# A hybrid HGRN2, attention and mixture-of-experts layer: the scheduler orders each engine's instructions by its detailed time model

## The chip, the cores and the metric

The kernel runs on one core of one Trainium2 chip. The metric is the device time of one execution in microseconds (us), the median over the runs shown. Engines: PE is TensorE's matmuls and PEld its weight loads, DVE is VectorE, ACT is ScalarE, POOL is GpSimd, SP is SyncE, which here issues almost all DMAs.

## The reference, cut to what matters

One layer over 256 latent tokens, with 256 context tokens as a prefix, and a width of 1024, in float32:

```python
u_lat = modulate(rmsnorm(x, g[0]), m_lat[0], m_lat[1])      # m = silu(c) @ w_mod + b_mod
y_lat = token_mixer(u_lat, u_ctx, ...)                       # HGRN2 (8 heads, 2 directions) and attention
x = x + m_lat[2] * rmsnorm(y_lat, g[1])
t = modulate(rmsnorm(x, g[2]), m_lat[3], m_lat[4])
logits = t @ router_w + router_b                             # top 4 of 32 experts, softmax over the 4
for e in range(N_EXPERTS):
    h = t @ w_up[e] + b_up[e]                                # 1024 -> 2048
    a = glu * sigmoid(1.702 * glu) * (lin + 1.0)             # both clamped at 7
    out = out + combine[:, e:e + 1] * (a @ w_down[e] + b_down[e])
x = x + m_lat[5] * rmsnorm(out, g[3])
```

The token mixer projects latent and context tokens by `w_in` (1024 x 8704), runs the recurrence and the attention, gates the two results, and multiplies by `w_branch` and `w_out`. Each expert's weights are 8 MB up and 4 MB down; all 32 are read once.

## The kernel before

The program is written as straight Python code over tiles, and is traced in that order. Three stages follow one another.

**The mixer.** Weights come in slabs of 1 MB (`slab`, L224, its transfer at L227) into three buffers with the tag `raw`. ACT and DVE split each half of a slab into a high and a low float32r part (L239, L240; two buffers, tag `hl`), and PE multiplies high by high, high by low and low by high (`mm3`, L247, L250, L251). Small dependent chains run between these: the gates and the scan of a pair of HGRN heads (`hgrn_pair`, four times), and the heads of the attention (`attn_head`, eight times: scores, maximum on DVE, exponential on ACT at L675, a product on DVE at L677, transposes on PE at L680, a split again). Between the heads stand the gated branches (`branch`: a sigmoid on ACT at L699). ACT has one table of functions at a time; where the function's table is not the one it holds, an ACT_TABLE_LOAD stands ahead of the instruction.

**Routing.** The last product with `w_out` leads through the second norm, the logits, the top 4 and the position of each token in its expert's list (L804 to L832).

**The experts.** Four experts at a time, the chosen tokens (64 at most for each) are gathered by a one-hot product (`gather`, L918, L922). For expert e, `up` loads four pieces of 2 MB (`wu`, L887, seven buffers over three tags) and multiplies (L953 for the bias, L963: 64 matmuls), then the gate is computed on DVE and ACT (L939 to L943). `down` of the expert before loads four pieces of 1 MB (`wd`, L894, six buffers) and multiplies (L990: 32 matmuls), copies on ACT (L993) and adds into the accumulators on PE (L997). `transposed` turns the gate's result (L977 on PE, L979 on ACT), and `scatter_weights` makes the weights of the sum (L931, L933, L935). The loop in program order:

```python
for e in range(NE - 1):
    a = up(e, xe, part if e == 0 else None)
    ...
    if before is not None:
        down(e - 1, before)
    before = transposed(e, a)
    if e % 4 == 3: ...          # gather the next four
down(NE - 2, before)
with tc.If(state["most"] > CAP): ...      # L1020: experts with more than 64 tokens, not taken here
e = NE - 1
row_bcast(g3, misc, mod[:, 0, 40:48], gT[:, 24:32], "b")     # L206 on DVE, L208 on PE, L214 on ACT
aT = transposed(e, up(e, xe))
```

Behind the branch comes expert 31, ahead of it in program order a row broadcast of the last gain (`row_bcast`), and then the last norm and the output.

**What sets the order.** Leaving `with tile.TileContext(nc)` starts the scheduler. It simulates the traced program on a model of the machine; whenever an engine's queue can take another instruction, it gives it the ready one that stands earliest in the program, and a tile gets a buffer when one of its tag is free. The order that comes out of this simulation is fixed in the program; on the chip every queue runs in that order and waits on semaphores. What is inside `tc.If` is one unit, and nothing is moved across it. `tc.keep_in_program_order` pins a few instructions (some first matmuls of a group, and the preloads of ACT's tables at L125). So a model of time decides only which ready instruction goes first.

## Time and profile before

| | us |
|---|---|
| median of 3 runs | 1460.55 (1459.64 to 1463.08) |
| the profiled execution | 1461.97 |
| its span, first to last instruction | 1460.4 |
| PE busy in the span | 1361.9 (93%) |
| DVE, ACT busy | 506.3, 360.6 |
| read from HBM | 479.15 MB |

The span is what the profile shows; 1.57 us of the execution's own time lie around it. Start times in the rows are us from the start of the span, durations of single instructions in the groups are ns. A row's bracket tells how long the engine sat idle before it, and what ended that.

### The profile page before, as it was taken

How to read it: one execution, taken by the hardware profiler on the slowest of the kernel's cores; microseconds unless marked ns; L12 is line 12 of the kernel's file. 1: busy time of each engine (PE TensorE's matmuls, PEld its weight loads, DVE VectorE, ACT ScalarE, POOL GpSimd, SP SyncE). 2: the span in 40 equal slices, each digit the busy share in tenths (PEclk: the TensorE clock that was granted, in tenths of full speed). 3: DMA queues.
4: the chain of work that ended last, by engine and by line, in shares of the span. 5: the costliest groups of instructions: out<-in, count | busy, mean ns of one | idle time of the engine just before them, and what ended most of it. 6: DMA issues, size and time to landing. Idle time of an engine off the chain costs nothing. (4 is left out here: it accounts for less than half of the span.)

```text
span 1460.4 us, 18959 instructions
## 1 busy us (share of the span) xinstructions
PE 1361.9 (93%) x8151; PEld 762.6 (52%) x8151; DVE 506.3 (35%) x916; ACT 360.6 (25%) x648; POOL 4.2 (0%) x16
## 2 busy tenths in 40 slices
PE   6999999999999999999999999999999999999976
PEld 3789788898899844553333333333333333333322
DVE  4688877778865521111111110111011111101012
ACT  5445444456554410100010010011010110101001
POOL 0000000000000000000000000000000000000000
PEclk9999999999999999999999999999999999999998
DMA  9544343246659599999999999999999999999992
GB/s 343 169 140 150 118 145 110 70 145 231 221 203 343 220 341 391 427 426 425 423 426 426 426 423 424 426 426 425 423 427 424 426 424 425 427 424 425 424 407 88
DMA packets 97553, 481.53 MB, mean 330 GB/s; under 512 B 6692, under 2 KB 57352, under 8 KB 63160
## 3 DMA queue, kind: packets, MB, share of 16 engines
q1 hardware_dynamic: 96560, 479.25, 81.8%
q8 instruction: 66, 1.08, 0.3%
q10 hardware_dynamic: 776, 0.84, 0.2%
q14 instruction: 23, 0.19, 0.0%
q0 software_dynamic: 128, 0.16, 0.0%
HBM read 479.15 MB, written 1.08 MB: 329 GB/s over the span
## 5 line engine op out<-in xcount | busy, mean ns | idle before, releaser
L963 PE MATMUL pu<-wu,xe 128*64 128x512 f32 x2048 | 450.5, 595 | 0.0
L963 PEld LDWEIGHTS pu<-wu,xe 128*64 128x64 f32 x2048 | 162.9, 137 | 270.0 <-issue 246.3
L990 PE MATMUL py<-wd,aT 128*64 128x512 f32 x992 | 231.2, 599 | 0.0
L939 DVE TENSOR_SCALAR gl<-pu 128x512 f32<-128x512 f32 (+1 forms) x33 | 22.2, 675 | 485.7 <-PE pu L963 485.7
L990 PEld LDWEIGHTS py<-wd,aT 128*64 128x64 f32 x992 | 65.7, 136 | 117.5 <-issue 108.9
L940 ACT ACTIVATE sg<-gl 128x512 f32<-128x512 f32 (+1 forms) x33 | 20.2, 616 | 416.9 <-DVE gl L939 416.9
L997 PE MATMUL acc<-ysb,cw 64*128 64x512 f32 x248 | 61.6, 615 | 16.1 <-ACT ysb L993 15.4
L918 PE MATMUL pgx<-oh,xt 128*128 128x256 f32 x256 | 66.7, 400 | 9.1 <-ACT aT L979 4.4
L918 PEld LDWEIGHTS pgx<-oh,xt 128*128 128x128 f32 x256 | 44.9, 195 | 39.2 <-issue 19.3
L931 DVE TENSOR_SCALAR ow<-iota,posb,comb 128x128 f32<-128x128 f32 x64 | 19.5, 344 | 132.1 <-PE pcw L933 132.1
L922 DVE TENSOR_SCALAR xe<-pgx,aff,mod 128x256 f32<-128x256 f32 x32 | 17.4, 544 | 127.2 <-PE pgx L918 127.2
L247 PE MATMUL pf<-uh,hlf 128*128 128x512 f32 x128 | 51.8, 410 | 3.1 <-ACT hlf L239 3.1
L979 ACT COPY aT<-pat 128x512 f32<-128x512 f32 x32 | 18.8, 586 | 143.6 <-PE pat L977 143.2
L251 PE MATMUL pf<-uh,hlf 128*128 128x512 f32 x128 | 52.8, 414 | 0.1
L250 PE MATMUL pf<-ul,hlf 128*128 128x512 f32 x128 | 51.9, 406 | 0.0
L997 PEld LDWEIGHTS acc<-ysb,cw 64*128 64x128 f32 x248 | 21.3, 186 | 52.4 <-ACT ysb L993 37.4
L993 ACT COPY ysb<-py 128x512 f32<-128x512 f32 x31 | 18.2, 586 | 117.6 <-PE py L990 117.6
L977 PEld LDWEIGHTS pat<-ident,gl 128*128 128x128 f32 x128 | 19.8, 205 | 46.0 <-issue 34.9
L977 PE MATMUL pat<-ident,gl 128*128 128x128 f32 x128 | 30.6, 327 | 12.0 <-DVE gl L943 12.0
L247 PE MATMUL pga<-uh,hlga 128*128 128x256 f32 x128 | 36.9, 288 | 1.7 <-ACT hlga L239 1.7
L251 PE MATMUL pga<-uh,hlga 128*128 128x256 f32 x128 | 36.3, 284 | 1.0 <-DVE hlga L240 1.0
L247 PE MATMUL pv<-hli,uh 128*128 128x256 f32 x128 | 36.5, 285 | 0.0
(387 smaller groups left out, 2142.7 us busy)
## 6 DMA issues: line engine op xcount, KB each, us to landing
wu<-in_w_up_dram SPq DMA_DIRECT2D x128, 2048.0 KB, 27.3
wd<-in_w_down_dram SPq DMA_DIRECT2D x124, 1024.0 KB, 18.4
wm<-in_w_mod_dram SPq DMA_DIRECT2D x16, 1024.0 KB, 4.9
wm<-in_w_mod_dram SPq DMA_DIRECT2D x16, 512.0 KB, 10.2
wf<-in_w_in_dram SPq DMA_DIRECT2D x8, 1024.0 KB, 5.2
wga<-in_w_in_dram SPq DMA_DIRECT2D x8, 1024.0 KB, 5.2
wwb<-in_w_branch_dram SPq DMA_DIRECT2D x8, 1024.0 KB, 6.4
wi<-in_w_in_dram SPq DMA_DIRECT2D x4, 1024.0 KB
```

The costliest lines, as they stand in the source:

```text
L247: i = pe.matmul(o, a[0], b[0], start=k == 0 and opens, stop=False)
L250: pe.matmul(o, a[0], b[1], start=False, stop=False)
L251: pe.matmul(o, a[1], b[0], start=False, stop=k == KT - 1 and closes)
L918: pe.matmul(pg, pairs(xt[:, tt], k), oh[:, tt].rearrange("p e s -> p (e s)"), start=tt == 0, stop=tt == 1)
L931: dve.tensor_scalar(ow[:, tt], view(iota, [[0, 2], [1, CAP]]), posb[:, tt, e:e + 1], comb[:, tt, e:e + 1], op0=ALU.is_equal, op1=ALU.mult)
L939: dve.tensor_scalar(gl, glu_ps, 7.0, None, op0=ALU.min)
L940: act.activation(sg, gl, AF.Sigmoid, scale=1.702)
L963: pe.matmul(pu[i][hf * CAP:(hf + 1) * CAP], lhs, wt[:, k % 2, i * 1024 + hf * 512:i * 1024 + (hf + 1) * 512], start=False, stop=k == KT - 1)
L977: pe.transpose(pt[:, b * P:(b + 1) * P], pairs(a[:], b), ident)
L979: act.copy(aT.rearrange("p a b -> p (a b)"), pt)
L990: pe.matmul(py[n * CAP:(n + 1) * CAP], aT[:, k % 4, (k // 4) * CAP:(k // 4 + 1) * CAP], wt[:, i, n * 512:(n + 1) * 512], start=k == 0, sto ...
L997: pe.matmul(acc[tt][n], cw[r, tt * P:(tt + 1) * P], ysb[r], start=False, stop=False)
```

## The change

One argument is given to the tile context. The simulation that orders the instructions then runs on the library's detailed model in place of its plain one. The detailed model lets transfers share the DMA engines, follows TensorE's clock, and treats the parts of an instruction (issue, read, write-back, the way of a semaphore) apart; it counts every table of ACT as loaded. No instruction, tile, buffer count or size in the kernel's text is changed; the order of every engine's queue, SP's and POOL's among them, may be.

```diff
-    with tile.TileContext(nc) as tc:
+    with tile.TileContext(nc, schedule_with_timeline_sim=True) as tc:
         hybrid_layer(tc, *args)
```

## Rows read from the trace of the kernel before

**Rows 1.** The page: busy time of each engine, then 40 slices of the span.

```profile
PE 1361.9 (93%) x8151; PEld 762.6 (52%) x8151; DVE 506.3 (35%) x916; ACT 360.6 (25%) x648; POOL 4.2 (0%) x16
...
GB/s 343 169 140 150 118 145 110 70 145 231 221 203 343 220 341 391 427 426 425 423 426 426 426 423 424 426 426 425 423 427 424 426 424 425 427 424 425 424 407 88
```

**Rows 2.** Windows: busy us (x instructions) of each engine, clock, DMA share, GB/s.

```profile
27.00:500.00 473.00, 462.84 (x4072) 412.81 (x4073) 348.28 (x558) 235.89 (x406) 2.21 (x5) 0.99 0.51 175
300.00:400.00 100.00, 93.94 (x728) 88.70 (x727) 82.69 (x140) 60.45 (x116) 0.00 (x0) 1.00 0.60 202
480.00:500.00 20.00, 20.00 (x164) 19.27 (x164) 9.83 (x15) 8.32 (x23) 0.00 (x0) 1.00 0.33 115
500.00:514.00 14.00, 10.63 (x53) 6.67 (x52) 11.01 (x51) 8.03 (x22) 0.49 (x1) 1.00 0.86 311
514.00:553.00 39.00, 38.83 (x168) 18.61 (x168) 5.74 (x12) 5.10 (x8) 0.50 (x1) 1.00 0.94 353
553.00:600.00 47.00, 47.00 (x220) 23.45 (x218) 6.54 (x12) 4.13 (x8) 0.00 (x0) 1.00 0.96 400
560.00:1410.00 850.00, 796.03 (x3590) 303.24 (x3586) 116.10 (x212) 86.10 (x160) 0.00 (x0) 1.00 1.01 425
```

**Rows 3.** Timeline of PE, second expert, then expert 30 and its neighbours.

```profile
539.69 14.11 PE L963 MATMUL pu<-wu,xe 128*64 128x512 f32 x64
...
1372.65 13.95 PE L963 MATMUL pu<-wu,xe 128*64 128x512 f32 x64
1386.44 1.89 PE L990 MATMUL py<-wd,aT 128*64 128x512 f32 x8
...
1393.06 0.44 PE L933 MATMUL pcw<-ident,ow 128*128 128x128 f32 x2 [0.73 <-ACT aT L979]
```

**Rows 4.** Groups of PE, 560 to 1410 us: busy, mean ns, idle before, releasers.

```profile
L977 PE MATMUL pat<-ident,gl 128*128 128x128 f32 x120 | 29.0, 329 | 9.9 <-DVE gl L943 9.9
...
L933 PE MATMUL pcw<-ident,ow 128*128 128x128 f32 x60 | 13.1, 300 | 14.6 <-ACT aT L979 14.6
```

**Rows 5.** DMA issues of the page, then waits of PE, 500 to 1410 us.

```profile
wu<-in_w_up_dram SPq DMA_DIRECT2D x128, 2048.0 KB, 27.3
wd<-in_w_down_dram SPq DMA_DIRECT2D x124, 1024.0 KB, 18.4
...
PE acc L997 <- ACT ysb L993: 15.4, 21, 0.7
```

**Rows 6.** Timeline of SP near the end, then the tile wu's landing, 1300 to 1410 us.

```profile
1347.38 5.29 SPq L887 DMA_DIRECT2D wu<-in_w_up_dram  x2
...
DMA to landing us min/median/max: 27.9/29.5/30.0
```

**Rows 7.** Timeline behind the branch: DVE, then PE.

```profile
1408.53 1.02 PE L997 MATMUL acc<-ysb,cw 64*128 64x512 f32 x4
...
1414.67 1.29 DVE L206 TENSOR_TENSOR rbdb<-ident,rbcb 128x512 f32<-128x512 f32 x2 [25.28 <-PEq L1020]
...
1415.42 3.78 PE L208 MATMUL rbpb<-rbdb,ones 128*128 128x512 f32 x4 [5.87 <-DVE rbdb L206]
...
1419.13 1.06 PE L953 MATMUL pu<-bu,sel 96*64 96x512 bf16 x4
```

**Rows 8.** Timeline of ACT at the start, then its groups, 330 to 430 us.

```profile
9.10 1.28 ACT L220 ACT_TABLE_LOAD   x1
...
10.39 0.48 ACT L220 ACTIVATE rs<-ssq,epsc 128x1 f32<-128x1 f32 x2
...
24.70 1.58 ACT L300 ACTIVATE xnT<-xnT,mod,aff 128x256 f32<-128x256 f32 x3 [0.99 <-DVE aff L295]
26.19 1.03 ACT L239 CAST hlf<-wf 128x1024 fp32r<-128x1024 f32 x1
...
L699 ACT ACT_TABLE_LOAD x4 | 5.1, 1283 | 0.1
L675 ACT ACT_TABLE_LOAD x3 | 3.8, 1283 | 0.1
```

## The prediction, made before the changed kernel was built

> **What bounds the kernel now.** I began with the page. PE is busy 93% of the span, and from slice 17 of 40 on the read rate stands at 423 to 427 GB/s [rows 1]. The first half is therefore PE's, and in the second two resources may run level, so stages are read next, by windows [rows 2]. From 27 to 500 us PE is busy 462.84 of 473 us. That leaves 10.16 us of gaps, and in the worst 100 us of it 6.06. DVE and ACT have 348.28 and 235.89 us of work there, so they have room to be served in another order. From 500 to 514 us PE is busy 10.63 of 14 us and DVE 11.01: a short dependent chain. From 560 to 1410 us the read rate is 425 GB/s at a DMA share of 1.01, with PE busy 796.03 of 850 us. The granted clock is 0.99 to 1.00 wherever it is listed, so I take the duration of a matmul as fixed.
>
> Which of the two bounds the experts is settled by the timeline of PE. The second expert's up-product begins at 539.69 us and expert 30's at 1372.65 [rows 3]; 832.96 / 29 = 28.72 us for each. The transfers of one expert, four of 2048 KB and four of 1024 KB [rows 5], are 12.58 million bytes, which at 425 GB/s take 29.6 us. PE thus runs a little faster than its weights come and eats up a lead of about 29 x 0.9 = 25 us. How much is left? The last two pieces of expert 30 are issued by 1347.38 + 5.29 = 1352.67 us, and such a piece lands 29.5 us later (median) [rows 6], at 1382.2. PE comes to the last of four pieces at about 1372.65 + 0.75 x 13.95 = 1383.1 [rows 3]. So **the lead is gone just when the loop ends**: 0.9 us are left. This is the reading on which the forecast turns. A wait taken out of PE's loop gains about 1 us in all, as the weights then come last; a wait put in costs its whole length, for every expert.
>
> **The change part by part.** It removes no instruction and adds none except, perhaps, table loads of ACT, which follow from the order. What it moves is the place of any instruction in its queue. Which ones move, the trace of before cannot show, so each stage is bounded from both sides. The sum stands against the profiled execution, 1461.97 us, which is 1.42 above the median of 1460.55. I call changes under 0.2%, 2.9 us, no difference, about what a measurement of this kernel can tell.
>
> *Start, ahead of 27 us.* ACT runs the last products of the normalization up to 26.19 us, then the cast that the first projection waits for, 1.03 us [rows 8]. If the cast goes ahead of them, PE can start up to 1 us earlier; if another such cast gets in front, 1 us later. I take 0 (-1.0 to +1.0).
>
> *The mixer, 27 to 500 us.* No reorder gains more than PE's 10.16 us of gaps [rows 2]. At worst I let all of it run at the rate of its worst stretch: 473 x 6.06 / 100 = 28.7 us of gaps, so 28.7 - 10.2 = +18.5. An order made with a finer model should see the short chains (score, exponential, product, transpose) with truer lengths and fill a quarter of the gaps: **-2.5**, near the gain's end since 98% of the stretch is full already and small errors of order are absorbed by DVE's 125 us and ACT's 237 us of idle time.
>
> *The transition, 500 to 514 us.* One chain; at most 14 - 10.63 = 3.4 us to gain or, taken the same, to lose [rows 2]. I take 0. A chain has one order.
>
> *SP's and POOL's queues.* Both may be reordered. SP's weights leave when a buffer comes free: the rate of 115 GB/s from 480 to 500 us, with 353 behind it [rows 2], I read as buffers still held by the mixer, which program order decides and time does not. POOL has 2.21 us of work in the mixer and small transfers. I take 0 for both. If the mixer gave its buffers up early enough to keep the stream at 425 GB/s from 514 on, 39 x (1 - 353/425) + 47 x (1 - 400/425) = 6.6 + 2.8 = 9.4 us more lead would be there.
>
> *The experts.* PE's largest waits are for the copy of the down-product (15.4 us, up to 0.7 each), for the copy of the transposed gate (14.6) and for the gate (9.9) [rows 4, 5]. Putting other matmuls in front of the waiting ones would hide them. The gain is the lead, 0.9, say **-1.1** with the earlier end of the copies (at best -1.1 - 9.4 = -10.5, with the stream kept full). A loss: one more wait per expert for an ACT copy, 0.73 us as in the timeline [rows 3], for 31 experts: +22.6. Queued behind such a wait is everything of PE, 64 up-matmuls first. I stay near the gain, as each wait of this kind is already in the order of before, so the model must find a second one.
>
> *Behind the branch.* PE ends its last sum at 1408.53 + 1.02 = 1409.55 us and stands for 5.87 us, as DVE comes to the row broadcast at 1414.67, released by the branch on PE's queue. Then PE runs the broadcast for 3.78 us ahead of expert 31's first matmul at 1419.13 [rows 7]. The up-product does not need the broadcast. With it behind, PE could start when DVE now does: 1419.13 - 1414.67 = up to 4.4 us gained. A model of time in which DVE's product and its semaphore take longer would let the bias matmuls, ready at once, go first. Half of it: **-2.2** (-4.4 to 0).
>
> *ACT's tables.* From 330 to 430 us ACT loads tables seven times, 1283 ns each, in front of sigmoids (L699) and exponentials (L675) in turn; at 9.10 us the next instruction starts 1.29 us behind such a load's start, at its end [rows 8]. The detailed model takes every table as held, so nothing in it keeps exponentials together. I take 0 for my forecast and price the rest as a rival. The Trainium skill, "ScalarE: Activation LUTs", section "What ACT_TABLE_LOAD costs", gives about 1.28 us for the load and a drain of about 1.38 us with it, 2.66 us for each switch; by it each added load would cost twice what I use. The trace shows the load and no gap behind it at 9.10 us [rows 8], so the trace decides here.
>
> The sum: 0 - 2.5 + 0 - 1.1 - 2.2 = -5.8; 1461.97 - 5.8 = 1456.2 for a profiled execution, and 1460.55 - 5.8 = **1454.8** for the median.
>
> **The rivals.**
>
> *One more wait for each expert* (0.22). Place: between PE and ACT in the loop, at the copies of L979 and L993. If the detailed model has the weights come later than they do, PE stands idle in the simulation, so it is given the transposes and sums the moment they are ready. On the chip, where the weights are there, PE then reaches them early and waits. For it: the lead falls to 0.9 us, so a model even slightly slower at transfers finds the loop bound by them throughout. Against it: such waits are in the order of before already, 0.7 us each [rows 5]. Price: 31 x 0.73 = 22.6, giving 1460.55 + 22.6 = 1483. It decides the sign from 5.8 + 2.9 = 8.7 us on, 0.28 us for each expert, since it first has to undo my other gains.
>
> *Exponentials and sigmoids in turn* (0.16). Place: ACT's queue in the eight heads and branches. If each head's exponential ends up between sigmoids of the branches, there are up to 16 loads in place of 7: 9 x 1.283 = 11.6 us of ACT. ACT is busy 60.45 of 100 us there, so half of it may be hidden from PE: about +6, giving 1466. For it: the loads already alternate, 4 and 3. Against it: PE's order there is mostly filled by slab products, which need no table. The rule of the Trainium skill, "ScalarE: Activation LUTs", section "Table sets: the hidden batching unit", that work is to be grouped by table set speaks for this rival; no run here shows yet what an order blind to them does.
>
> *No change that counts* (0.22). The two models may give nearly the same order, since the ready instruction that stands earliest goes first in both, and 64 up-matmuls stand in the same row either way. Or gain and loss cancel. Then 1460.5, within 2.9 us.
>
> **How the numbers follow.** The forecast, faster by over 2.9 us, has 0.40: its own range is 1446 to 1457.6, the lower end from the mixer's whole 10.2 us with the tail's 4.4. No change has 0.22 and the two slower cases 0.22 + 0.16 = 0.38. The likeliest single case is the forecast. The range goes down to 1445, the forecast's end with the start's 1.0, and up to 1482, which takes in the table rival whole and the wait rival up to its full price; what is left out is that price with losses of the mixer on top, and the stream kept full with everything else gained.
>
> **What would show it.** Mixer: PE's busy time in the windows from 27 us to the end of the last product by `w_out`; right if its gaps are below 10 us, wrong if above 13. Experts: expert 1's up-product to expert 30's, 28.7 us each if right; 29.0 or more, with longer waits for ACT's copies in the list of PE's waits, is the first rival. Tail: bias matmuls of L953 ahead of L208 in PE's timeline, and its idle time below 5.87 us. Tables: seven loads in front of L699 and L675 over the whole mixer's heads; ten or more is the second rival. The prediction fails if a stage's first instruction on SP, a weight held back behind a transfer that waits for a buffer, moves the start of the expert stream; the rate from 480 to 600 us would show that.

## The result, and the profile after

The changed kernel takes 1518.99 us (median of 4 runs, 1517.28 to 1520.06), against 1460.1 for the kernel before, measured beside it: a ratio of 1.0391, 95% interval 1.0373 to 1.0409. It is 59 us slower, outside the range that was forecast. No instruction was added on PE, DVE, ACT or POOL; only the order differs, on every engine and on SP.

From the page of the changed kernel, busy time of each engine and the read rate in 40 slices (a slice is now 37.9 us):

```profile
PE 1389.1 (92%) x8151; PEld 768.1 (51%) x8151; DVE 504.9 (33%) x916; ACT 359.7 (24%) x648; POOL 3.8 (0%) x16
...
GB/s 338 155 111 167 140 112 133 73 129 236 214 29 274 288 269 356 423 427 426 426 424 426 426 424 425 425 425 427 426 424 423 426 426 425 426 424 426 424 249 70
```

[Rows 1] have no slice like the twelfth here: 29 GB/s, from 417 to 455 us. The windows of the changed kernel show what PE did there:

```profile
27.00:500.00 473.00, 431.46 (x3740) 385.62 (x3741) 328.06 (x529) 217.20 (x368) 1.77 (x5) 0.95 0.45 151
...
420.00:440.00 20.00, 13.39 (x77) 10.63 (x75) 13.04 (x29) 8.66 (x18) 0.00 (x0) 0.91 0.14 47
440.00:460.00 20.00, 14.39 (x70) 10.93 (x70) 10.44 (x23) 6.91 (x15) 0.00 (x0) 0.78 0.00 1
...
480.00:500.00 20.00, 17.62 (x133) 17.22 (x132) 9.98 (x12) 7.31 (x9) 0.00 (x0) 0.91 0.65 209
500.00:553.00 53.00, 50.85 (x382) 45.89 (x382) 29.70 (x82) 26.75 (x58) 0.51 (x1) 0.97 0.87 332
553.00:600.00 47.00, 47.00 (x198) 19.99 (x199) 9.48 (x18) 5.98 (x10) 0.50 (x1) 0.99 0.76 292
560.00:1410.00 850.00, 807.83 (x3571) 298.79 (x3572) 121.52 (x224) 86.69 (x161) 0.50 (x1) 0.98 1.00 421
```

Against [rows 2], PE's gaps from 27 to 500 us grew from 10.16 to 41.5 us, its work there fell from 4072 matmuls to 3740, and the mixer runs on past 500 us: the first up-product of expert 0 starts at 554.15 us, where it started at 514.05. From 560 us on the stream is nearly what it was, 421 GB/s against 425, and (1414.26 - 578.69) / 29 = 28.81 us go to an expert against 28.72. Then 17 more microseconds go at the end, as shown below.

**Bytes and landings.** By 600 us the kernel before has moved 129.0 MB (215 GB/s in the window from 0 to 600), the changed one 111.6 (186 GB/s). The missing 17.4 MB at 425 GB/s are 40.9 us; the last piece of the stream (`wu` of L887 or `wd` of L894) lands at 1461.3 us where it landed at 1421.8, 39.5 later. Expert 31's own down weight (`wl`, L902) comes behind it, at 1485.1 and 1433.0 us, and is no part of this count. From that last landing to the end of the span are 55.8 us, against 38.6. So the spans' difference, **56.7 us, is 39.5 of a stream that lags and 17.2 behind its end**. The same two numbers, read from each run's trace, place the other kernels of this study (MB by 600 us are the rate of that window times 600 us):

| kernel | MB by 600 us | expert 0 starts | last piece lands | of | span | span - landing |
|---|---|---|---|---|---|---|
| before | 129.0 | 514.0 | 1421.8 | wu | 1460.4 | 38.6 |
| changed | 111.6 | 554.2 | 1461.3 | wd | 1517.1 | 55.8 |
| e1 | 108.6 | 561.1 | 1468.0 | wd | 1526.6 | 58.6 |
| e2 | 108.6 | 552.6 | 1471.0 | wu | 1508.1 | 37.1 |
| e4 | 129.6 | 512.5 | 1419.7 | wd | 1473.5 | 53.8 |
| e5 | 124.8 | 520.8 | 1431.0 | wd | 1490.9 | 59.9 |
| e6 | 123.6 | 518.2 | 1432.8 | wu | 1469.4 | 36.6 |
| e9 | 111.6 | 551.7 | 1462.7 | wu | 1498.9 | 36.2 |
| e10 | 116.4 | 540.7 | 1449.4 | wd | 1508.4 | 59.0 |
| e11 | 113.4 | 546.3 | 1456.5 | wd | 1513.0 | 56.5 |
| e12 | 127.2 | 513.6 | 1426.9 | wu | 1470.2 | 43.3 |
| e13 | 126.0 | 515.0 | 1427.7 | wu | 1464.4 | 36.6 |

1421.8 + (129.0 - MB) / 0.425 gives each landing within about 2 us (e7, told below, is the exception: 91.8 MB, 1509.3 by the rule, 1526.5 measured). And what is left behind the landing is 36 to 43 us where an up weight is last, 54 to 60 where a down weight is. Small steps in this table say little: beside e5 to e13 the kernel before had medians of 1465.8 to 1466.6 us, and e13, which costs nothing against that, lands 5.9 us behind the first row.

**Why the mixer is late.** First, where PE's 31.4 us of new gaps stand. Windows of the changed kernel, and the second wait of PE in them:

```profile
27.00:100.00 73.00, 63.66 (x446) 52.73 (x447) 45.81 (x86) 29.32 (x42) 0.00 (x0) 0.88 0.48 164
100.00:300.00 200.00, 198.41 (x1979) 177.75 (x1978) 148.78 (x226) 91.35 (x151) 1.77 (x5) 1.00 0.39 128
300.00:420.00 120.00, 105.08 (x902) 98.64 (x900) 91.33 (x146) 64.61 (x125) 0.00 (x0) 0.96 0.57 186
...
59.30 2.07 PE L247 MATMUL pf<-uh,hlf 128*128 128x512 f32 x4 [4.51 <-DVE uh L301]
```

In the same windows PE was busy 70.70, 198.38 and 113.76 us before. So 7.0 us of the new gaps come ahead of 100 us (most of it a first projection that starts 2.6 us later, and the wait of 4.51 us shown), none from 100 to 300, 8.7 from 300 to 420, 12.2 from 420 to 460 and 3.5 behind that. Two changes of order can be seen. The first is in the recurrent pairs; ACT's timeline in the changed kernel, first pair:

```profile
99.98 0.62 ACT L457 COPY ke<-ks 128x512 f32<-128x512 f32 x1
104.84 1.05 ACT L239 CAST hlf<-wf 128x1024 fp32r<-128x1024 f32 x1 [4.24 <-PE pf L251]
106.17 0.62 ACT L457 COPY ke<-ks 128x512 f32<-128x512 f32 x1 [0.28 <-PE pl L462]
...
111.39 1.04 ACT L239 CAST hlf<-wf 128x1024 fp32r<-128x1024 f32 x1
112.33 0.62 ACT L552 COPY fl<-fl 128x512 f32<-128x512 f32 x1
112.97 0.62 ACT L457 COPY ke<-ks 128x512 f32<-128x512 f32 x1
116.99 1.05 ACT L239 CAST hli<-wi 128x1024 fp32r<-128x1024 f32 x1 [3.41 <-PE pf L251]
```

and in the kernel before:

```profile
87.55 0.62 ACT L457 COPY ke<-ks 128x512 f32<-128x512 f32 x1
89.87 0.62 ACT L457 COPY ke<-ks 128x512 f32<-128x512 f32 x1 [1.70 <-DVE ks L490]
91.41 0.62 ACT L457 COPY ke<-ks 128x512 f32<-128x512 f32 x1 [0.91 <-PE pl L462]
94.53 1.05 ACT L239 CAST hlf<-wf 128x1024 fp32r<-128x1024 f32 x1 [2.51 <-PE pf L251]
```

The copy L457 opens a level of the scan. It came about every two microseconds; now it stands behind a cast of half a slab that waits for PE to free a buffer, and comes every six. The five batches of L462 reach from 98.5 to 125.3 us, before from 86.9 to 96.9. The four pairs end (L513) at 158.7, 222.9, 282.4 and 331.8 us, before at 117.3, 176.8, 232.8 and 291.9. The scale of the queries (L654), for which every head waits, comes at 363.1, not 336.1. PE loses no time by that from 100 to 300 us, since it runs other slabs meanwhile. The second change follows: slabs of the gated branches have gone ahead, and when the last heads come next to nothing is left to run between them. PE's timeline of the changed kernel, heads 5 and 6:

```profile
440.10 0.63 PE L680 MATMUL ppt<-ident,pr 128*128 128x128 f32 x4 [2.08 <-DVE pr L677]
441.40 0.58 PE L685 MATMUL poa<-ph,vah 128*128 128x256 f32 x1 [0.68 <-ACT ph L239]
441.78 0.63 PE L668 MATMUL pss<-khT,oab 128*128 128x512 f32 x1
...
445.59 0.39 PE L669 MATMUL pss<-klT,oab 128*128 128x512 f32 x1
...
449.09 0.63 PE L680 MATMUL ppt<-ident,pr 128*128 128x128 f32 x4 [2.08 <-DVE pr L677]
```

A bare head takes 9 us, and PE waits for DVE and then for ACT in each. Before, heads at nearly the same pace (9.6 us) had slab matmuls in every gap, as here behind the transposes, where no wait is shown:

```profile
391.04 0.63 PE L680 MATMUL ppt<-ident,pr 128*128 128x128 f32 x4
391.43 0.36 PE L247 MATMUL pga<-uh,hlga 128*128 128x256 f32 x1
```

The last head's product (L685) starts at 460.4 us, before at 421.3.

**SP** issues nothing for 44 us there, since its next transfer wants a buffer that the attention holds (timeline of SP in the changed kernel, then its longest wait):

```profile
418.21 0.37 SPq L227 DMA_DIRECT2D wga<-in_w_in_dram  x1
462.57 1.29 SPq L887 DMA_DIRECT2D wu<-in_w_up_dram  x3
470.66 0.38 SPq L227 DMA_DIRECT2D wwb<-in_w_branch_dram  x1
...
SPq L887 <- DVE plo L240: 41.4, 1, 41.4
```

Three pieces of expert 0 stand ahead of a slab that PE needs. It looks like the cause. It is not (e1, e12).

**The end.** SP's queue now issues expert 30's down weight behind expert 31's up weight. PE in the changed kernel:

```profile
1461.32 1.94 PE L990 MATMUL py<-wd,aT 128*64 128x512 f32 x8 [0.26 <-DMA wd<-in_w_down_dram]
1463.99 1.99 PE L997 MATMUL acc<-ysb,cw 64*128 64x512 f32 x8 [0.74 <-ACT ysb L993]
1471.20 1.06 PE L953 MATMUL pu<-bu,sel 96*64 96x512 bf16 x4 [5.22 <-PEq L1020]
1472.03 4.33 PE L963 MATMUL pu<-wu,xe 128*64 128x512 f32 x10
1476.28 1.98 PE L208 MATMUL rbpb<-rbdb,ones 128*128 128x512 f32 x4
1478.20 12.23 PE L963 MATMUL pu<-wu,xe 128*64 128x512 f32 x54
```

Expert 30's product takes the last landing; then comes the branch; then expert 31's whole up-product, whose weights had landed by 1451.38. Before, the last landing, at 1421.8 us, fell into that up-product:

```profile
1419.99 14.47 PE L963 MATMUL pu<-wu,xe 128*64 128x512 f32 x64
```

It ended 12.7 us behind the landing; now it ends 29.1 behind.

### The profile page after: what moved, and what is told of

Same layout as the page of the kernel before. It is cut to its first block, busy times and chain, and to the rows that moved or that the text cites. A ratio compares the mean times of both kernels' runs of the same rounds, so it can differ in the third digit from the quotient of the medians.

```text
span 1517.1 us, 19110 instructions
## 1 busy us (share of the span) xinstructions
PE 1389.1 (92%) x8151; PEld 768.1 (51%) x8151; DVE 504.9 (33%) x916; ACT 359.7 (24%) x648; POOL 3.8 (0%) x16
## 5 line engine op out<-in xcount | busy, mean ns | idle before, releaser
L963 PE MATMUL pu<-wu,xe 128*64 128x512 f32 x2048 | 485.4, 600 | 1.0 <-DMA wu<-in_w_up_dram 1.0
L963 PEld LDWEIGHTS pu<-wu,xe 128*64 128x64 f32 x2048 | 152.4, 137 | 262.0 <-issue 248.4
L990 PE MATMUL py<-wd,aT 128*64 128x512 f32 x992 | 243.2, 614 | 25.8 <-DMA wd<-in_w_down_dram 25.8
L990 PEld LDWEIGHTS py<-wd,aT 128*64 128x64 f32 x992 | 73.1, 140 | 155.6 <-issue 122.8
L922 DVE TENSOR_SCALAR xe<-pgx,aff,mod 128x256 f32<-128x256 f32 x32 | 17.4, 544 | 230.3 <-PE pgx L918 230.3
L918 PE MATMUL pgx<-oh,xt 128*128 128x256 f32 x256 | 73.8, 417 | 4.9 <-ACT xe L920 2.6
L979 ACT COPY aT<-pat 128x512 f32<-128x512 f32 x32 | 18.7, 584 | 212.2 <-PE pat L977 212.2
L920 ACT ACTIVATE xe<-pgx,mod,aff 128x256 f32<-128x256 f32 x32 | 18.0, 564 | 128.6 <-PE pgx L918 128.6
L953 PE MATMUL pu<-bu,sel 96*64 96x512 bf16 x128 | 27.0, 394 | 14.8 <-DVE sg L942 9.2
L250 PE MATMUL pga<-ul,hlga 128*128 128x256 f32 x128 | 37.3, 291 | 0.0
```

Source lines behind the costliest of these rows:

```text
L250: pe.matmul(o, a[0], b[1], start=False, stop=False)
L918: pe.matmul(pg, pairs(xt[:, tt], k), oh[:, tt].rearrange("p e s -> p (e s)"), start=tt == 0, stop=tt == 1)
L953: pe.matmul(pu[i][hf * CAP:(hf + 1) * CAP], bl, bu3[:, i * 1024 + hf * 512:i * 1024 + (hf + 1) * 512], start=True, stop=False)
L963: pe.matmul(pu[i][hf * CAP:(hf + 1) * CAP], lhs, wt[:, k % 2, i * 1024 + hf * 512:i * 1024 + (hf + 1) * 512], start=False, stop=k == KT - 1)
L979: act.copy(aT.rearrange("p a b -> p (a b)"), pt)
L990: pe.matmul(py[n * CAP:(n + 1) * CAP], aT[:, k % 4, (k // 4) * CAP:(k // 4 + 1) * CAP], wt[:, i, n * 512:(n + 1) * 512], start=k == 0, sto ...
```

## The experiments

Orders were held by edges between instructions of one engine, which only say what goes first. A queue that is not held is ordered anew around those that are:

```python
def behind(tc, later, earlier):
    if earlier is not None:
        tc.add_manual_dep(later.ins, earlier.ins.name,
                          mybir.DependencyInfo(mybir.DependencyClass.NoSync, mybir.DependencyReason.DATA),
                          reason="order")
    return later
```

### SP's queue: e1 to e4

e1, on the changed kernel, in `up_piece` (`last[nm]` keeps the transfers of `slab`):

```diff
-        nc.sync.dma_start(wt, w_up[0, e, j * 256:(j + 1) * 256].rearrange("(p i) f -> p (i f)", i=2))
+        d = nc.sync.dma_start(wt, w_up[0, e, j * 256:(j + 1) * 256].rearrange("(p i) f -> p (i f)", i=2))
+        behind(tc, d, last["wb13"] if e == 0 else None)
```

> Detailed model, with one order pinned: the four pieces of expert 0's up weight stand on SP behind the last branch slab (wwb of branch 1, 3) and no longer ahead of the slabs. Theory A (SP's queue: three up pieces that wait for the attention's buffers hold the mixer's slabs back from 418 to 462 us, and PE runs the last heads with nothing between): slabs go on being issued after 418 us, PE is busy over 95% of 420 to 460 us, the mixer ends about 20 us earlier, 1519 - 20 = about 1499. Theory B (the loss is in PE's own order of the mixer, heads late and bare whatever SP does): PE's gaps from 420 to 460 us stay, 1515 to 1522.

Measured: 1525.93 us (ratio to before 1.0423, 1.0388 to 1.0459), no faster than the changed kernel (1.0373 to 1.0409), and a little above Theory B's range. Theory A falls here. SP's waits of e1 from 400 to 600 us say why:

```profile
SPq L227 <- DVE hlga L240: 64.7, 3, 51.3
SPq L887 <- PE pu L963: 38.0, 7, 10.8
```

The slab now at the head of the queue waits 51.3 us itself: its buffer is free once the slab ahead of it is split, and that waits for PE to use up the slabs of the second branch, which need the heads' results. PE's queue, not SP's, left the heads bare: PE is busy 27.2 of the 40 us from 420 on, 27.8 in the changed kernel.

e2 holds every transfer of `up_piece` and `down_piece` behind the one traced before it (`last["x"] = behind(tc, d, last.get("x"))`); e3 has both edits.

> Detailed model, with the weights of the experts pinned on SP to program order (four up pieces of an expert, then four down pieces of the expert before, to the end; expert 31's up weight behind expert 30's down weight). Theory A (the end costs 16.5 us of its own, because expert 30's down weight is issued last, behind expert 31's up weight, and the branch makes PE finish expert 30 first): the last landing to the last up-matmul falls from 29 to about 13 us, 1519 - 16.5 = about 1502. Theory B (everything is the late stream, the end follows whatever comes last): 1515 to 1522.

> Detailed model with both pins. Theory A: the two add, 1519 - 20 - 16.5 = about 1483; what is left over the kernel before (about 22 us) is PE's order in the mixer, in which it was 18 us behind at 420 us already. Theory B (SP's order is no cause): 1515 to 1522.

Measured: e2 1509.6 us (1.0318, 1.0286 to 1.0349), e3 1512.06 (1.0347, 1.0315 to 1.038). Both lie between their theories. In e2 the span behind the last landing fell from 55.8 to 37.1 us as Theory A said, but the landing came 9.7 us later: program order holds a down piece, whose buffer is free, behind an up piece whose buffer isn't. Half of the 18.7 gained was lost again. SP's wait for that up piece in e2:

```profile
SPq L887 <- PE py L251: 28.5, 1, 28.5
```

e3 is no faster than e2, so e1's edit gains nothing here either.

e4 tests the end by itself, on the kernel before (`last[f"wd{e}{q}"]` keeps the transfers of `down_piece`):

```diff
+        _ = [behind(tc, last[f"wd30{q}"], d) for q in range(4) if (e, j) == (NE - 1, 3)]
```

> Plain model, with the end of SP's queue alone as the changed kernel has it: expert 31's up weight ahead of expert 30's down weight. All other queues are those of the kernel before. Theory A: expert 30's down-product waits for the last landing, then the branch, then expert 31's up-product comes whole: about +14 to +17, 1476. Theory B: the order of two loads at the end does not matter as the same bytes land at the same time, 1460.

Measured: 1475.78 us (1.0116, 1.0065 to 1.0167), 14.3 above the median beside it: Theory A. Every other queue runs in the order of before. PE in e4:

```profile
1412.44 9.25 PE L990 MATMUL py<-wd,aT 128*64 128x512 f32 x32 [14.20 <-DMA wd<-in_w_down_dram]
1422.43 1.99 PE L997 MATMUL acc<-ysb,cw 64*128 64x512 f32 x8 [0.74 <-ACT ysb L993]
```

The last piece of the stream lands even 2 us earlier than before, and PE idles 14.20 us for it with the other expert's up weight there since 1409.8 us.

### Mixer against experts: e5, e9, e6

The program is traced and scheduled twice: once with the plain model, whose order is then pinned, engine by engine, on part of a second trace under the detailed model. `k` counts traced instructions; 4662 is where the experts begin.

```diff
+    first, _ = program(inputs, False)
+    order = [i.name for b in first.main_func.blocks if "_layer" in b.name for i in b.instructions]
+    nc, arrays = program(inputs, True, order)
...
+        if e in ("PE", "Activation", "DVE", "Pool", "SP") and k < 4662:
+            if e in ahead:
+                tc.add_manual_dep(i, ahead[e],
+                                  mybir.DependencyInfo(mybir.DependencyClass.NoSync, mybir.DependencyReason.DATA),
+                                  reason="order")
+            ahead[e] = name
```

> Detailed model, but every engine's instructions ahead of the experts (mixer and routing) are held in the order of the kernel before; the experts stay as the detailed model orders them. Theory C (about 40 us are lost in the mixer: its recurrent scans and attention heads come later in the queues, the heads end bare, and the expert weights' stream starts 40 us late; another 14 to 16.5 us are the order of the last loads): 1461 + 14 to 16.5 = 1475 to 1478. Theory D (the experts' own order costs most, and the late mixer would be made good by a stream that runs full anyway): 1500 or more.

e9 has `k >= 4662`; e6 is e5 with e2's edit.

> The reverse: detailed model, but every engine's instructions of the experts and of the end are held in the order of the kernel before; mixer and routing stay as the detailed model orders them. Theory C: 1461 + 40 = about 1500 to 1503. Theory D: 1480 or less.

> As the first of these (mixer in the order of before), and the experts' weights on SP in program order as in e2; the other engines' order in the experts stays the detailed model's. Theory C: both costs gone, 1458 to 1466. Theory D: what is left of PE's order in the experts shows, 1480 or more.

Measured: e5 1491.51 us (1.0171, 1.0137 to 1.0205), e9 1502.3 (1.0251, 1.0216 to 1.0285), e6 1474.67 (1.0074, 1.0043 to 1.0106). e9 is where Theory C put it: the mixer's order alone costs 2.5%, some 37 us. e5 missed both theories: the experts' order costs 1.7%, 25 us, not 14 to 16. The two, 2.51 + 1.71 = 4.22%, make up the whole of 3.91% and a little more. e6 kept 0.74% (0.43 to 1.06), 8 us between the medians and 11 by the ratio, that Theory C did not expect. Its SP queue stands at the start of the stream: one transfer of L887 waits 31.7 us for a buffer that L786 reads, with expert 0's down pieces behind it. e13, next, shows that the 25 us of e5 are all SP's. The end takes about 14 of them by e4, or 21 by e5's own row, which has 59.9 us behind the landing against 38.6; the rest, 4 to 11 us, is a stream that fills later. The runs do not settle that split.

### The experts without SP: e13

As e5, with `k < 4662 or e == "SP"`.

> Detailed model, with the mixer and routing of all engines and the whole of SP's queue held in the order of before: the detailed model orders only PE, DVE, ACT and POOL in the experts and at the end. If the prediction's terms for the loop (-1.1) and for the end (-2.2) were right: 1457 to 1460, with the waits for the copies of L993 and L979 shorter. If the detailed order of the loop costs by itself (what e6 kept over the kernel before): 1467 to 1475.

Measured: 1466.08 us beside 1465.84 for the kernel before, ratio 1.0 (0.998 to 1.0019). PE's waits from 500 to 1410 us in e13:

```profile
PE pu L963 <- DMA wu<-in_w_up_dram: 39.1, 35, 2.0
PE acc L997 <- ACT ysb L993: 13.6, 19, 0.7
```

The waits for L979 and for the gate of [rows 4] are gone from the list, and 39.1 us of waits for weights have come in their place. No time changed: what PE no longer waits for inside, it waits for at the transfers. PE's order among the experts is not quite that of the changed kernel here, as it was made around another SP; what the run shows is that with the mixer and SP's queue held the detailed order of the other engines costs nothing.

### Where in the mixer: e7, e8, e10, e11

e7 is e5 with `e == "Activation"` alone. e8 pins one thing on ACT of the changed kernel: `behind(tc, c, last["km"] if nm in ("f11", "f12", "f13") else None)` for the cast `c` of a slab, where `last["km"]` is the copy L457.

> Detailed model, with ACT's queue alone held in the order of before ahead of the experts; PE, DVE, SP and POOL are ordered by the detailed model around it. Theory E (within C: ACT is the cause; the copies for the scan's levels, L457, stand behind casts of slabs, L239, that wait for PE to free a buffer, so that one level of the scan takes the time of half a slab, 6 us, where it took 2): the scans and with them the heads come back to their times, 1478 to 1495. Rival F (PE's own order puts slabs ahead of the scan's levels, whatever ACT does): 1510 to 1522.

> Detailed model with one pin on ACT: the casts of the second forget slab of the next pair stand behind the last copy of the scan's levels (L457) of the pair before, for all pairs; nothing else is held. Theory H (the scans are the root: one level in 6 us in place of 2 delays each pair's end by 40 us, and the attention with it): the five levels' batches of pair 0 stand within 15 us in place of 27, the attention ends 15 to 30 us earlier, 1490 to 1505. Theory G (the late scans are absorbed; what costs is the order of the attention part, where slabs of the gated branches go ahead of the heads and the last heads stand bare): 1512 to 1522.

Measured: e7 1584.48 us (1.0804, 1.0771 to 1.0836); e8 1528.51 (1.0423, 1.0403 to 1.0444). Both miss. e7 fits neither theory: here an order of ACT made for another order of PE is worse than either whole, expert 0 starting at 619.8 us. e8 did bring the levels of the second and third pair together (L462's first four batches from 168.3 to 174.6 us, in place of 169.4 to 186.4), but the pairs end at 153.4, 218.3, 279.8 and 340.6, no earlier at the end. As the other queues were ordered anew around this pin, e8 alone proves little; but PE has no new gap from 100 to 300 us in the changed kernel either. The slow levels go with the lateness; that they set it is not shown.

e10 pins all engines for `k < 2492` (to the end of the recurrent pairs), e11 for `2492 <= k < 4662`.

> Detailed model, with every engine's instructions up to the end of the four recurrent pairs held among themselves in the order of before; attention, branches, routing and experts as the detailed model orders them. Theory H: the attention ends when it did before, 1488 to 1497. Theory G: the last heads stay bare, 1508 to 1522.

> The complement: every engine's instructions from the key and value projections to the routing's end held among themselves in the order of before; the recurrent pairs as the detailed model orders them. Theory H: 1508 to 1522. Theory G: the heads have their slabs between them again and end near 424 us, 1488 to 1497.

Measured: e10 1512.78 us (1.0326, 1.0296 to 1.0356), e11 1514.41 (1.0311, 1.0276 to 1.0346). Each gives back under 1%: e10 falls in Theory G's range and e11 in Theory H's, so neither theory holds. In e10 the first three pairs end as before (118.3, 177.9, 233.6 us) but the fourth comes at 318.3, as the attention's slabs go ahead of it, and the last heads stand bare until 448. In e11 the heads have slabs between them (0.2 us of gaps from 420 to 460), yet begin late, and end at 449 as well; its gaps stand elsewhere, 11.6 us from 100 to 300, where the changed kernel has 1.6. Either half of the detailed order is enough for expert 0 to start 27 to 32 us late; both together make 40. Which choice of the model starts it was not found.

### The start of the stream: e12

Plain model, the order of before on SP, with expert 0's four transfers taken out and put behind the last slab of `w_out`:

```diff
+    late = [n for n in order if "wu0_" in text.get(n, "")]
+    order = [n for n in order if n not in late]
+    at = 1 + max(k for k, n in enumerate(order) if "wwo3" in text.get(n, ""))
+    order[at:at] = late
```

> Plain model and the queues of before, but the four up pieces of expert 0 stand on SP behind the last slab of w_out, so that the experts' stream starts at about 465 us in place of 424, as late as in the changed kernel (462); PE's mixer is not touched. Theory S (the start of the stream sets the end, 40 us late is 40 us lost): 1495 or more. Theory M (the early start only fills seven buffers that then wait for the mixer to end, which the 115 GB/s from 480 to 500 us speak for; what counts is when the mixer ends and gives its buffers up): 1460 to 1470.

Measured: 1471.91 us (1.0047, 1.0027 to 1.0067), 6 us above the median beside it, just over Theory M's range and far from S. PE's order in the mixer is that of before. The windows of e12:

```profile
480.00:500.00 20.00, 20.00 (x161) 18.95 (x160) 9.95 (x17) 7.81 (x20) 0.00 (x0) 1.00 0.99 419
500.00:514.00 14.00, 10.63 (x41) 5.98 (x41) 9.44 (x48) 8.03 (x22) 0.49 (x1) 0.88 1.01 423
```

Where [rows 2] have 115 and 311 GB/s, e12 has 419 and 423: a stream that starts 42 us late makes nearly all of it good, because the early start only filled buffers that then stood full. What it can't make good is a mixer that ends late and gives up its own buffers late. In the table the landing follows the start of expert 0 in step, +40 and +39.5 us in the changed kernel, +27 and +28 in e10.

## Why the prediction was wrong, point by point

- **The mixer, -2.5 with +18.5 at worst: the step that failed.** It measured about +37 us (e9). Expert 0 starts 40.1 us later, of which 30.7 are gaps of PE and 9.4 the same matmuls run slower. By its own sign (wrong above 13 us of gaps) it failed plainly, with 41.5 from 27 to 500 us. The bound took the rate of gaps in the worst stretch of the old order as the worst a new order could do. That rate belongs to an order, not to the work: from 420 to 460 us the new one leaves 12.2 us of gaps in 40, five times the rate of [rows 2]. "Small errors of order are absorbed by idle time" failed too: DVE and ACT had their 125 and 237 us idle, but the chains between them run one link after the other, and PE needs other work at hand just then.
- **SP's queue, 0: the second step that failed.** "Which program order decides and time does not" was taken from a queue whose order came from a simulation of time. It costs about 25 us (e5 against e13), 14 or more of them at the end (e4). My statement that nothing moves across the branch was wrong for SP: the kernel before already had expert 31's first two pieces ahead of it, the changed one all four, and expert 30's down weight behind them.
- **That the lead is gone when the loop ends, and that a wait taken out gains nothing: right**, and shown by e13, where waits for weights took the place of those taken out. The loop's -1.1 and the end's -2.2 measured as 0.0 together (within 0.2%, 2.9 us); -1.1 alone could not be told from nothing.
- **One more wait for each expert, +22.6: did not come.** The list of PE's waits from 500 to 1410 us in the changed kernel has less of them than [rows 4] and [rows 5]:

```profile
PE py L990 <- DMA wd<-in_w_down_dram: 18.4, 3, 15.9
...
PE acc L997 <- ACT ysb L993: 5.9, 8, 0.7
PE pcw L933 <- ACT aT L979: 2.9, 4, 0.7
```

What is new in it are waits for weights, one of them long. The average pace hides it, as the stream runs on (424 GB/s from 1110 to 1127 us):

```profile
1122.03 3.68 PE L990 MATMUL py<-wd,aT 128*64 128x512 f32 x8 [15.93 <-DMA wd<-in_w_down_dram]
```

- **Table loads: did not come.** L699 has four and L675 two in the changed kernel's mixer, against four and three [rows 8]. The whole run has 22 loads before and after. The Trainium skill, "ScalarE: Activation LUTs", section "Table sets: the hidden batching unit", wants calls batched by table set; by this count the change neither made nor broke such batches, though the model is blind to them.
- **The end, -2.2: right in the order, wrong in the gain.** The bias matmuls did go ahead of L208, and from the last sum's end to the first up-matmul PE now takes 6.1 us, not 10.4. But from that sum to the up-product's end it takes 24.5 against 24.9: 0.5 us, see below.
- **The start, 0 within 1.0:** the first projection came at 29.87 us, not 27.27, 2.6 later.
- **What would make it wrong** was named, a weight on SP held back behind a transfer that waits for a buffer, and the rate from 480 to 600 us did fall, from 327 to 296 GB/s by the windows. But e1 and e12 show that such a hold of expert 0's first pieces costs little; the rate fell because the mixer was late (e9, with the old order of the experts, has the same 111.6 MB by 600 us). A sign was right and its reading was not.

The forecast's fault beneath these: I bounded a new order by small steps away from the old one. The change replaces all the orders at once.

## What to carry to other kernels

A list scheduler's order is only as good as its model's choice of the next ready instruction, and a model with more detail can choose worse: price a change of it by what the stretches have to hide (dependent chains with nothing else at hand, buffers that one stage hands to the next), not by the gaps that the old order left. Two numbers place such a program: the bytes moved when the stream becomes full, and what has to follow the last landing. To find what an order costs, pin all the queues of one stage to the old order; pinning one engine alone (e7) makes a third order that tells little of either.

## What the runs showed that was not expected

- PE pays for its gaps a second time. In the bare heads the granted clock is 0.91 and 0.78 and the same matmul L668 or L669 takes 0.63 us where it takes 0.39; PE's busy time over the whole run is 27.2 us more for the same 8151 matmuls: 9.4 ahead of expert 0's first up-product, where it delays what follows, and 18.2 among the experts, where PE waits for transfers anyway. There the granted clock is 0.50 from 1110 to 1127 us, inside the wait of 15.93 us and just behind it.
- At the end that undoes a gain. Behind 5.87 us of idle time the four matmuls L208 took 3.78 us [rows 7]; placed after ten up-matmuls they take 1.98. But it is then the up-matmuls that run slowly, ten in 4.33 us, and the end comes only 0.5 us sooner.
- A stream started 42 us late cost 6 us (e12), and two weights exchanged at the end of it, with its last piece landing 2 us earlier, cost 14 (e4): here, which tile lands last counts for more than when the stream starts.
